# A two-layer hybrid block on one core: residual stream with tokens on partitions instead of features

## The chip, the core and the metric

The kernel runs on one core of a Trainium2 chip. The metric is the device time of one execution in microseconds (us); the figure for the kernel before is the median of three timed runs. A profile is one further execution, recorded instruction by instruction; its span runs from the first to the last instruction.

## What is computed

Two layers work on 256 latent tokens `x` and 256 context tokens `ctx`, 1024 features each. A layer is a half feed-forward step, a token mixing (gated linear attention, a 2D Fourier transform, latent attention, merged by gates) and a second half feed-forward step. The last layer drops the context after its mixing. Each of the six steps has this frame, cut from the reference:

```
def _rmsnorm(x, g):
    xf = x.astype(jnp.float32)
    y = xf * lax.rsqrt(jnp.mean(xf * xf, axis=-1, keepdims=True) + EPS)
    return (y * g.astype(jnp.float32)).astype(x.dtype)
def _half_ffn(x, mod, g_pre, g_post, wg, wu, wd):
    shift, scale, gate = mod
    h = _rmsnorm(x, g_pre) * (1 + scale) + shift
    y = (jax.nn.silu(h @ wg) * (h @ wu)) @ wd
    return x + 0.5 * gate * _rmsnorm(y, g_post)
```

`wg` and `wu` are 1024 x 2816, `wd` is 2816 x 1024, and the output projection of the mixing, `w_out`, is 1024 x 1024. `shift`, `scale` and `gate` come from a modulation, one vector for the context and one for the latents.

## The kernel before, in words

All activations lie with features on the partitions: 8 tiles of 128 features by 512 tokens, the context in columns 0 to 255, the latents in 256 to 511. Every product is done in float32r with both operands split into a high and a low part, so one block of 128 x 128 weights costs three matmuls: weights-high by activations-high, weights-high by activations-low, weights-low by activations-high (`acc`). The weights are stationary, the tokens move: 512 columns for both streams, 256 for one.

Weights stream through `Stream`: SP issues loads of 512 KB into four raw buffers, ACT copies the high part (line 140), DVE subtracts for the low part (line 141), in pieces of 512 columns, up to 8 or 9 pieces ahead of use. The modulation vectors (`mod_chunk`, line 292) are made by DVE beside the first two feed-forward steps, from weights that pass through the same four buffers.

The six steps are called f0, mixer and f1 of layer 0 and layer 1 here; each ends in `down` (the product by `wd`, tiles named `d`, or by `w_out`, tiles named `o`). `down` makes one output tile of 128 features at a time. The last one (two for `o`) is made first for the context half and then for the latent half, 256 columns each, so that the norms of the context half lie beside the products of the latent half; `dense_pair` does the same with the first two or four tiles of the next step. Between the two lie, per half, `postnorm` and `prenorm`: sums of squares over the partitions by fp32 matmuls against ones (tiles `png`, `pnc`, `qnc`), a power of -0.5 on POOL (`pnr`, `qnr`), a broadcast of the result over the partitions by another matmul (`pnb`, `qnb`), then DVE, ACT and POOL apply it. In layer 1 only the latents pass `o` and f1, 256 columns at a time.

Each engine takes its instructions in a fixed order, which a scheduler writes when the program is built; an instruction that waits holds up all behind it on its engine.

Of the kernel before, what the change touches and what calls it, by code (L numbers as in the profile page):

```python
# [16 lines left out]
L = 2  # L17
# [15 lines left out]
PER_ATT = 4  # L33

# [6 lines left out]
# chunks in the order in which each direction's state passes them, but for the last  # L41
# [3 lines left out]
# columns of the tables of the 2D transform  # L45
# [136 lines left out]
class K:  # L182
# [10 lines left out]
    def pools(self, ctx):  # L193
        P = lambda **k: ctx.enter_context(self.tc.tile_pool(**k))
        self.const = P(name="const", bufs=1)
        self.raw_p = P(name="raw", bufs=RAW_BUFS)
        self.c_p = P(name="c", bufs=C_BUFS)
        self.f_p = P(name="f", bufs=3)
        self.s_p = P(name="s", bufs=7)
        self.t_p = P(name="t", bufs=3)  # L200
        self.v_p = P(name="v", bufs=6)
        self.mm_p = P(name="mm", bufs=3, space=PSUM)
        self.aux_p = P(name="aux", bufs=5, space=PSUM)
# [4 lines left out]
    def rows(self, n, name, dt=F32):  # L208
        """n tiles [128, 512], two in each buffer."""
# [24 lines left out]
    def setup(self):  # L234
# [5 lines left out]
        self.x = c.tile([128, NT, 512], F32, name="x")  # L240
        nc.scalar.dma_start(self.cond, self.io["cond"])
        for j in range(4):
            nc.sync.dma_start(self.x[:, 2 * j:2 * j + 2, :], self.io["x"][:, 2 * j:2 * j + 2, :])
# [14 lines left out]
    def cond_rows(self):  # L258
        """silu of both conditions along the free axis, for the modulation."""
# [7 lines left out]
    def mod_finish(self, l, i, m, ts=slice(0, NT)):  # L267
        """Adds the bias and folds the weights of the norms into scale and gate."""
# [12 lines left out]

    def mod_chunk(self, l, i):
        """One of the nine modulation vectors of both conditions, feature-major: [128, tile, cond]."""
        nc = self.nc
        m = self.const.tile([128, NT, 2], F32, name=f"m{l}_{i}")
        rs = [1] if l == L - 1 and i > 4 else [0, 1]
        if len(rs) == 1:
            nc.vector.memset(m, 0.0)
# [9 lines left out]
        self.modv[l][i] = m  # L298

    def first_mod(self, t, m2, ps):  # L300
        """Shift and scale of the first norm, for one tile of features."""
# [18 lines left out]
    def start(self):  # L320
        """The first norm and the first tiles of the first FFN, one tile of features at a time, as
        their modulation arrives."""
# [3 lines left out]
        m2 = [self.const.tile([128, NT, 2], F32, name=f"m0_{a}") for a in range(2)]  # L326
        self.modv[0][0:2] = m2
        sqs = []
        for j in range(4):
            sq, xj = self.c([2, 512], "xsq"), self.x[:, 2 * j:2 * j + 2, :]  # L330
            if j % 2:
                nc.vector.tensor_tensor(sq, xj, xj, ALU.mult)
            else:
                nc.scalar.activation(sq, xj, AF.Square)
            sqs += [sq[:, 0, :], sq[:, 1, :]]
        tot = self.sums(sqs, "pn", 512)
        self.first_mod(0, m2, mps)
        bc = self.rstd_of(tot, 1.0 / D, "pn")
        pg = [self.mm("pg") for _ in range(M0)]
        pu = [self.aux("pu") for _ in range(M0)]  # L340
        for t in range(NT):
            if t:
                self.first_mod(t, m2, mps)
            for hf in range(2):
                self.pre_tile(0, 0, hf, t, bc[:, 256 * hf:256 * hf + 256])
# [9 lines left out]
    def rstd(self, sqs, invd, name):  # L355
        """1/sqrt(mean + eps) of the tokens on all partitions; sqs: squares to be summed."""
        return self.rstd_of(self.sums(sqs, name), invd, name)

    def sums(self, sqs, name, n=256):
        """Sums over the features, tokens on the partitions."""  # L360
        nc = self.nc
        col = self.ones[:, 0:1]
        if len(sqs) == NT:
            gps = self.aux(name + "g")
            for j in range(NT):
                g = 32 * (j % 4)
                nc.tensor.matmul(gps[g:g + 32, 0:n], lhsT=self.ones[:, 0:32], rhs=sqs[j], start=j < 4, stop=j >= 4)
            part = self.t(name + "s") if n == 256 else self.s(name + "s")
            nc.vector.tensor_copy(part, gps[:, 0:n])
            sqs, col = [part], self.cst[:, C_32:C_32 + 1]  # L370
        cps = self.aux(name + "c")
        for c in range(n // 128):
            for i, sq in enumerate(sqs):
                nc.tensor.matmul(cps[:, c:c + 1], lhsT=sq[:, 128 * c:128 * c + 128], rhs=col,
# [19 lines left out]
    def pre_stats(self, hf):  # L394
        nc = self.nc
        sl = slice(256 * hf, 256 * hf + 256)
        sqs = []
        for j in range(4):
            sq = self.s("xsq", (2, 256))
            nc.scalar.activation(sq, self.x[:, 2 * j:2 * j + 2, sl], AF.Square)  # L400
            sqs += [sq[:, 0, :], sq[:, 1, :]]
        return self.rstd(sqs, 1.0 / D, "pn")

    def pre_tile(self, l, which, hf, t, bc):
# [5 lines left out]
        if t % 2 == 0 or t == 1:  # L410
            nc.vector.scalar_tensor_tensor(tmp, self.x[:, t, sl], A, bc, ALU.mult, ALU.mult)
            nc.scalar.activation(hi, tmp, AF.Identity, bias=B)  # L412
            nc.vector.scalar_tensor_tensor(lo, tmp, B, hi.bitcast(F32), ALU.add, ALU.subtract)
        else:
            nc.vector.tensor_tensor(tmp, self.x[:, t, sl], bc, ALU.mult)
            nc.scalar.activation(tmp, tmp, AF.Identity, bias=B, scale=A)
            nc.scalar.copy(hi, tmp)
            nc.gpsimd.tensor_tensor(lo, tmp, hi.bitcast(F32), ALU.subtract)  # L418

    def prenorm(self, l, which, hf):  # L420
        bc = self.pre_stats(hf)
        for t in range(NT):
            self.pre_tile(l, which, hf, t, bc)

    def postnorm(self, hf, out=False):
        nc = self.nc
        sl = slice(256 * hf, 256 * hf + 256)
        bc = self.rstd([q[:, sl] for q in self.ysq], 1.0 / D, "qn")
        for j in range(4):
            yj, xj = self.y[j][:, :, sl], self.x[:, 2 * j:2 * j + 2, sl]  # L430
            nc.vector.tensor_tensor(yj, yj, bc.unsqueeze(1).broadcast_to([128, 2, 256]), ALU.mult)
            (nc.vector if j >= 2 else nc.gpsimd).tensor_tensor(xj, xj, yj, ALU.add)
            if out:
                nc.sync.dma_start(self.io["out"][:, 2 * j:2 * j + 2, :], xj)
# [7 lines left out]
    def dense(self, key, rhi, rlo, t0, name):  # L442
        """One tile of 128 output features by the tokens from t0, over len(rhi) tiles of inputs."""
# [8 lines left out]
    def dense_pair(self, keys, t0, names):  # L452
        """Several tiles over the whole width, first for the context, then for the latent tokens."""
        if t0:
            return [self.dense(k, self.hi, self.lo, t0, n) for k, n in zip(keys, names)]
        out, blocks = [], []
        for key, n in zip(keys, names):
            self.W.unit(key, 1024)
            blocks.append([self.W.next() for _ in range(NT)])
            out.append((self.aux if len(out) % 2 and len(keys) > 3 else self.mm)(n))  # L460
        for hf in range(2):
            sl = slice(256 * hf, 256 * hf + 256)
            for ps, bl in zip(out, blocks):
# [789 lines left out]
```

## Time and profile before

| | |
|---|---|
| median of three runs | 2275.65 us (2273.53 to 2286.22) |
| span of the profiled execution | 2269.7 us |
| mean granted TensorE clock | 0.979 of full |
| busy: PE, DVE, ACT, POOL | 2174.9, 1325.8, 883.0, 254.2 us |
| read from HBM | 294.93 MB |

The profiled execution has no time of its own beside its span; the span lies 5.95 us under the median of the runs. PE's busy time counts overlapping matmuls once, each with its way through the array, so it tells that PE is rarely empty, not how fast it goes.

### The profile page before, as it was taken

The numbers are of one execution on the slowest core, as the hardware profiler recorded it, in microseconds if no ns is written. First come the engines' busy times: TensorE is split into PE (matmuls) and PEld (weight loads), VectorE is DVE, ScalarE is ACT, GpSimd is POOL, SyncE is SP. The second block draws the span as 40 slices with busy tenths as digits, with TensorE's granted clock in tenths as the row PEclk, the third lists the DMA queues.
The fourth block names the chain that finished last, engine by engine and source line by source line (L and its number), as shares of the span: only waits on it lengthen the run. The fifth ranks groups of instructions, "written<-read, shape, count | busy, mean of one in ns | idle before, by whom it ended". The sixth has DMA issues, their size and how long they took to land.

```text
span 2269.7 us, 34594 instructions
## 1 busy us (share of the span) xinstructions
PE 2174.9 (96%) x13686; PEld 1842.6 (81%) x13686; DVE 1325.8 (58%) x2568; ACT 883.0 (39%) x1759; POOL 254.2 (11%) x227
## 2 busy tenths in 40 slices
PE   7999999899999999999999999999998999998998
PEld 5788777677777788888888878888887788998998
DVE  4877687567665734377765553333225677665553
ACT  3332222454344523442232343323325445555452
POOL 0000001233120100200000020000002332101001
PEclk9999999899999999999999999999999999998999
DMA  8555466221111223245556623232321322453552
GB/s 300 192 182 197 159 202 207 86 93 57 41 60 56 88 81 111 75 158 176 195 197 218 214 77 112 75 111 71 119 90 47 121 69 89 152 183 129 186 188 92
DMA packets 87587, 298.23 MB, mean 131 GB/s; under 512 B 9664, under 2 KB 14016, under 8 KB 87424
## 3 DMA queue, kind: packets, MB, share of 16 engines
q1 hardware_dynamic: 85760, 291.54, 38.8%
q10 hardware_dynamic: 1664, 4.48, 0.6%
q8 instruction: 107, 1.75, 0.3%
q14 instruction: 56, 0.46, 0.1%
HBM read 294.93 MB, written 1.05 MB: 130 GB/s over the span
## 4 chain that ended last, share of the span: by engine, by line
PE 66%; DVE 13%; DMA 9%; ACT 4%; issue 4%; POOL 3%; ACTq 0%; DVEq 0%; POOLq 0%
DMA raw<-wmod 8%; PE d L438 5%; PE d L440 5%; PE d L439 5%; PE pu L439 4%; PE pu L440 4%; PE pu L438 3%; PE pg L439 3%; PE pg L440 3%; PE pg L438 3%; DVE junk L292 3%; PE ga L440 3%; PE ga L438 3%; PE ga L439 3%; DVE raw L292 3%
## 5 line engine op out<-in xcount | busy, mean ns | idle before, releaser
L141 DVE TENSOR_TENSOR w<-raw,w 128x512 fp32r<-128x512 f32 (+1 forms) x840 | 536.5, 685 | 246.9 <-ACT w L140 244.0
L140 ACT CAST w<-raw 128x512 fp32r<-128x512 f32 (+1 forms) x840 | 460.8, 605 | 244.7 <-DMA raw<-wd 73.3
L292 DVE SCALAR_TENSOR_TENSOR raw<-raw,cbc 128x1024 f32<-128x1024 f32 x128 | 159.7, 1248 | 50.7 <-DMA raw<-wmod 48.5
L292 DVE SCALAR_TENSOR_TENSOR junk<-raw,cbc 128x1024 f32<-128x1024 f32 x96 | 120.2, 1252 | 88.6 <-DMA raw<-wmod 88.4
L510 POOL TENSOR_TENSOR dq<-dq 128x512 f32<-128x512 f32 (+1 forms) x24 | 30.5, 1269 | 1143.2 <-ACT dq L483 1143.2
L543 DVE TENSOR_TENSOR sg<-sg,pu 128x512 f32<-128x512 f32 (+1 forms) x88 | 54.3, 618 | 155.2 <-PE pu L440 151.8
L483 ACT ACTIVATE dq<-d 128x512 f32<-128x512 f32 (+1 forms) x35 | 17.9, 511 | 175.4 <-PE d L440 175.4
L438 PE MATMUL ga<-h01h,w 128*128 128x512 f32 x192 | 76.0, 396 | 0.0
L542 ACT ACTIVATE sg<-pg 128x512 f32<-128x512 f32 (+1 forms) x88 | 47.5, 540 | 72.8 <-PE pg L440 72.8
L440 PE MATMUL ga<-h01h,w 128*128 128x512 f32 x192 | 75.4, 393 | 0.0
L439 PE MATMUL ga<-h01l,w 128*128 128x512 f32 x192 | 75.0, 391 | 0.0
L439 PE MATMUL pg<-h02l,w 128*128 128x512 f32 (+1 forms) x192 | 71.8, 376 | 1.7 <-POOL h02l L418 1.6
L438 PE MATMUL pu<-h02h,w 128*128 128x512 f32 (+1 forms) x192 | 72.5, 378 | 0.0
L439 PE MATMUL pu<-h02l,w 128*128 128x512 f32 (+1 forms) x192 | 72.3, 377 | 0.0
L440 PE MATMUL pu<-h02h,w 128*128 128x512 f32 (+1 forms) x192 | 72.3, 377 | 0.0
L440 PE MATMUL pg<-h02h,w 128*128 128x512 f32 (+1 forms) x192 | 72.0, 376 | 0.1
L438 PE MATMUL pu<-h10h,w 128*128 128x512 f32 (+1 forms) x192 | 72.0, 375 | 0.0
L439 PE MATMUL pg<-h10l,w 128*128 128x512 f32 (+1 forms) x192 | 71.5, 373 | 0.4 <-POOL h10l L418 0.4
L438 PE MATMUL pg<-h02h,w 128*128 128x512 f32 (+1 forms) x192 | 71.6, 376 | 0.2 <-ACT w L140 0.2
L439 PE MATMUL pu<-h10l,w 128*128 128x512 f32 (+1 forms) x192 | 71.7, 374 | 0.0
L438 PE MATMUL pg<-h00h,w 128*128 128x512 f32 x176 | 69.4, 394 | 2.4 <-ACT h00h L412 2.1
L440 PE MATMUL pu<-h10h,w 128*128 128x512 f32 (+1 forms) x192 | 71.7, 373 | 0.0
(528 smaller groups left out, 6208.9 us busy)
## 6 DMA issues: line engine op xcount, KB each, us to landing
raw<-wgu SPq DMA_DIRECT2D x170, 512.0 KB, 4.5
raw<-wmod SPq DMA_DIRECT2D x128, 512.0 KB, 4.3
raw<-win SPq DMA_DIRECT2D x92, 512.0 KB, 3.6
raw<-wd SPq DMA_DIRECT2D x64, 448.0 KB, 4.0
raw<-wd SPq DMA_DIRECT2D x32, 512.0 KB, 4.5
raw<-wm SPq DMA_DIRECT2D x16, 512.0 KB, 7.3
raw<-wbr SPq DMA_DIRECT2D x16, 512.0 KB, 3.6
raw<-wout SPq DMA_DIRECT2D x16, 512.0 KB, 4.5
```

Of the source, the lines that this page charges most:

```text
L140: nc.scalar.copy(hi, w)
L141: nc.vector.tensor_tensor(lo, w, hi.bitcast(F32), ALU.subtract)
L292: nc.vector.scalar_tensor_tensor(w if r else self.junk, w, 1.0, self.cbc[r], ALU.mult, ALU.mult, accum_out=m[:, t, r:r + 1])
L438: nc.tensor.matmul(ps, lhsT=hi, rhs=rhi, start=first, stop=False)
L439: nc.tensor.matmul(ps, lhsT=hi, rhs=rlo, start=False, stop=False)
L440: nc.tensor.matmul(ps, lhsT=lo, rhs=rhi, start=False, stop=last)
L483: nc.scalar.activation(sq[:, sl], ps[:, sl], AF.Square)
L510: nc.gpsimd.tensor_tensor(accq[:, t0:512], accq[:, t0:512], sq[:, t0:512], ALU.add)
L542: nc.scalar.activation(sg[:, t0:512], pg[:, t0:512], AF.Silu)
L543: nc.vector.tensor_tensor(sg[:, t0:512], sg[:, t0:512], pu[:, t0:512], ALU.mult)
```

## The change

The residual `x` is kept with tokens on the partitions: four tiles of 128 tokens by 1024 features. In `down` the activations are now the stationary operand and the weights move, 512 output features at a time: for each half `h` of the features and each of the 22 (or 8) input tiles, four token tiles (two in layer 1's `o` and last `d`) get three matmuls. The last `hold` input tiles of the second half are held back and done token tile by token tile, so that tiles 0 to 3 end one after the other. ACT squares a finished PSUM tile with a running sum along the free axis, DVE multiplies it by the gate, which now lies along the free axis and is fetched through DRAM (`gate_rows`). `residual` finishes a token tile: two small DVE steps with a power on POOL between, the update of `x`, the sum of squares of the new `x`, another power, and the normed rows `n`. These go back to features on partitions by transposes on PE (`turned`, `turn_tile`), and `pre_tile` applies scale and shift from PSUM. The matmuls for sums and broadcasts of these norms are gone. `dense_pair` now walks the input tiles outermost, issues the latent half's transposes and `pre_tile` (`self.late`) inside its context half, and takes three tiles instead of two at the start of a mixer.

```
+    def residual(self, j, ss, out):
+        r = self.norm_of(ss[:, 0:1], ss[:, 1:2])
+        sx = self.v("sx", 2)
+        for h in range(2):
+            sl = slice(512 * h, 512 * h + 512)
+            xj = self.x[:, j, sl]
+            nc.vector.scalar_tensor_tensor(xj, self.y[j][:, sl], r, xj, ALU.mult, ALU.add)
             if out:
...
+                nc.scalar.activation(self.sink[:, sl], xj, AF.Square, scale=D ** -0.5, accum_out=sx[:, h:h + 1])
...
+        r = self.norm_of(sx[:, 0:1], sx[:, 1:2])
+        n = self.c([D], f"n{j}")
+        nc.vector.tensor_scalar(n, self.x[:, j, :], r, None, ALU.mult)
+        return n
...
+        def mul(ps, kt, w, j):
+            sl = slice(128 * j, 128 * j + 128)
+            hi, lo = ahi[kt][:, sl], alo[kt][:, sl]
+            nc.tensor.matmul(ps, lhsT=hi, rhs=w[0], start=kt == 0, stop=False)
+            nc.tensor.matmul(ps, lhsT=hi, rhs=w[1], start=False, stop=False)
+            nc.tensor.matmul(ps, lhsT=lo, rhs=w[0], start=False, stop=kt == n - 1)
...
+        def evac(ps, j, h):
+            sl = slice(512 * h, 512 * h + 512)
+            nc.scalar.activation(self.sink[:, sl], ps, AF.Square, scale=D ** -0.5, accum_out=ss[j][:, h:h + 1])
+            nc.vector.tensor_tensor(y[j][:, sl], ps, g[j // 2][:, sl], ALU.mult)
...
+        for j in tiles:
+            for kt, w in held:
+                mul(ps[j], kt, w, j)
+            evac(ps[j], j, 1)
+            ns[j] = self.residual(j, ss[j], nxt is None)
+            if j == 2 and t0 == 0 and nxt:
+                turned = [self.aux("pt", (2, 256)) for _ in range(4)]
+                self.turn_tile(turned, 0, ns[0])
+            yield
...
+            if t0 == 0:
+                self.turn_tile(turned, 1, ns[1])
+                half(0, turned)
+            self.late = lambda: half(1, self.turned([ns[2], ns[3]]))
```

`norm_of` is a small DVE step and the power on POOL; `hold` is 6 in f0 and f1, 8 in the mixers.

At the seam from f0 to the mixer of layer 1, DVE's queue held these rows before. `qnv` belongs to the norm of the latent half of `d`'s last tiles, `dy` and `x` to the residual of the context half, `pnv` to its next norm, `h11l` is the low part of the mixer's input.

```order
L382 TENSOR_SCALAR qnv<-qnc 128x2
L141 TENSOR_TENSOR w_13740<-raw_13614,w_13740 128x512
L141 TENSOR_TENSOR w_13754<-raw_13646,w_13754 128x512
L141 TENSOR_TENSOR w_13769<-raw_13646,w_13769 128x512
L431 TENSOR_TENSOR dy_13016<-dy_13016,qnb 128x2x256
L431 TENSOR_TENSOR dy_13017<-dy_13017,qnb 128x2x256
L431 TENSOR_TENSOR dy_13018<-dy_13018,qnb 128x2x256
L431 TENSOR_TENSOR dy_13019<-dy_13019,qnb 128x2x256
L432 TENSOR_TENSOR x<-x,dy_13018 128x2x256
L432 TENSOR_TENSOR x<-x,dy_13019 128x2x256
L369 COPY pns<-png 128x256
L382 TENSOR_SCALAR pnv<-pnc 128x2
```

Now the same place on DVE reads, for the last two of the four token tiles (the first two stand ahead of it in the same way):

```order
L529 TENSOR_TENSOR dy_12838<-d,gr_12882 128x512
L445 SCALAR_TENSOR_TENSOR nv<-ss_12842 128x1
L457 SCALAR_TENSOR_TENSOR x<-dy_12838,nr,x 128x512 x2
L445 SCALAR_TENSOR_TENSOR nv<-sx 128x1
L466 TENSOR_SCALAR n_13607<-x,nr 128x1024
L529 TENSOR_TENSOR dy_12839<-d,gr_12882 128x512
L445 SCALAR_TENSOR_TENSOR nv<-ss_12843 128x1
L457 SCALAR_TENSOR_TENSOR x<-dy_12839,nr,x 128x512 x2
L445 SCALAR_TENSOR_TENSOR nv<-sx 128x1
L466 TENSOR_SCALAR n_13654<-x,nr 128x1024
L438 TENSOR_SCALAR pnt<-pt,m_4_9526,m_3_9203 128x256
L439 TENSOR_TENSOR h11l_13500<-pnt,h11h_13496 128x256
```

The whole chain of the latents' tiles 2 and 3 stands ahead of the first low part `h11l` of the context half; before, only the context half's own norms did.

On PE the last rows of `d` and the first of the mixer's pair at the same seam were, before:

```order
L387 MATMUL pnb<-cst,pnr 128x128 x2
L440 MATMUL d<-a20h_12941,w_13643 128x256
L438 MATMUL d<-a20h_12941,w_13643 128x256
L439 MATMUL d<-a20l_12942,w_13643 128x256
L440 MATMUL d<-a20h_12941,w_13643 128x256
L374 MATMUL qnc<-cst,dq 128x1 x4
L438 MATMUL zx<-h11h_13805,w_13657 128x256
```

and now, from the last three products of token tile 3 on:

```order
L522 MATMUL d<-w_13423,a20h_12761 128x512
L523 MATMUL d<-w_13423,a20h_12761 128x512
L524 MATMUL d<-w_13423,a20l_12762 128x512
L428 MATMUL pt<-cst,n_13572 128x128 x8
L428 MATMUL pt<-cst,n_13607 128x128 x2
L471 MATMUL zx<-h11h_13496,w_13440 128x256
L471 MATMUL zk<-h11h_13496,w_13472 128x256
L471 MATMUL zk<-h11h_13496,w_13480 128x256
L428 MATMUL pt<-cst,n_13654 128x128 x2
L472 MATMUL zx<-h11l_13500,w_13440 128x256
```

Between the last product of `d` and the first of the mixer there are no products left for PE to do, only transposes; the fp32 sums and broadcasts are gone.

## Rows read from the trace of the kernel before

**Rows 1.** The page, busy time by engine, with its share and instructions:

```profile
PE 2174.9 (96%) x13686; PEld 1842.6 (81%) x13686; DVE 1325.8 (58%) x2568; ACT 883.0 (39%) x1759; POOL 254.2 (11%) x227
```

**Rows 2.** Timeline of PE, `o` of layer 0: start us, us, what; ten products of 512:

```profile
902.75 0.39 PE L438 MATMUL o<-mh,w 128*128 128x512 f32 x1
...
904.79 0.39 PE L438 MATMUL o<-mh,w 128*128 128x512 f32 x1
```

**Rows 3.** Timeline of PE, last `d`: 23 products of 256:

```profile
2199.78 0.28 PE L438 MATMUL d<-a14h,w 128*128 128x256 f32 x1
...
2202.42 0.28 PE L439 MATMUL d<-a20l,w 128*128 128x256 f32 x1
```

**Rows 4.** Busy time (instructions) by engine, clock, DMA, at the five seams:

```profile
388.93:447.07 58.14, 48.01 (x309) 40.79 (x307) 37.94 (x73) 25.70 (x53) 16.29 (x15) 0.85 0.35 111
935.39:992.34 56.95, 51.79 (x369) 46.39 (x368) 31.12 (x60) 28.36 (x56) 14.69 (x15) 0.88 0.21 67
1315.56:1372.81 57.25, 51.89 (x398) 46.69 (x396) 36.77 (x68) 30.36 (x62) 14.98 (x15) 0.97 0.27 89
1695.15:1744.15 49.00, 41.22 (x309) 35.92 (x308) 27.88 (x55) 23.83 (x49) 14.59 (x15) 0.97 0.21 65
2051.31:2065.86 14.55, 7.39 (x38) 4.06 (x37) 6.23 (x12) 3.78 (x8) 3.91 (x4) 0.68 0.12 38
```

**Rows 5.** Groups of instructions by shape: busy us, mean ns of one:

```profile
L141 DVE TENSOR_TENSOR w<-raw,w 128x512 fp32r<-128x512 f32 x736 | 485.2, 702 | 227.7 <-ACT w L140 225.1
L543 DVE TENSOR_TENSOR sg<-sg,pu 128x512 f32<-128x512 f32 x66 | 45.2, 684 | 119.3 <-PE pu L440 116.3 <-ACT sg L542 2.9
L755 DVE SCALAR_TENSOR_TENSOR tg<-tg,br 128x512 f32<-128x512 f32 x24 | 16.5, 686 | 56.9 <-PE br L440 56.9
L1029 DVE TENSOR_SCALAR pr<-pr,rr 128x512 f32<-128x512 f32 x32 | 17.5, 546 | 0.2
L1029 DVE TENSOR_SCALAR pr<-pr,rr 128x256 f32<-128x256 f32 x16 | 5.6, 348 | 0.3
L415 DVE TENSOR_TENSOR pnt<-x,pnb 128x256 f32<-128x256 f32 x33 | 13.6, 413 | 0.8 <-POOL h02l L418 0.2 <-POOL h11l L418 0.2 <-POOL h10l L418 0.2
L483 ACT ACTIVATE dq<-d 128x512 f32<-128x512 f32 x21 | 12.5, 597 | 126.1 <-PE d L440 126.1
L1027 ACT ACTIVATION_READ_ACCUMULATOR pr<-sc,nb 128x1 f32 x48 | 9.2, 193 | 0.0
L400 ACT ACTIVATE xsq<-x 128x512 f32<-128x512 f32 x36 | 22.0, 629 | 30.8 <-POOL x L432 30.2 <-DVE x L432 0.5
L384 POOL TENSOR_TENSOR pnr<-pnv,cst 128x4 f32<-128x4 f32 x1 | 1.3, 1285 | 16.8 <-DVE pnv L382 16.8
L1047 PE MATMUL pt<-cst,pr 128*128 128x128 f32 x160 | 23.0, 275 | 1.3 <-DVE nb L1024 1.3
```

**Rows 6.** Timeline of all engines after the last product:

```profile
2257.98 0.28 PE L440 MATMUL d<-a20h,w 128*128 128x256 f32 x1
...
2259.66 0.16 DVE L382 TENSOR_SCALAR qnv<-qnc 128x2 f32<-128x2 f32 x1 [15.46 <-PE qnc L374]
2259.90 0.71 POOL L384 TENSOR_TENSOR qnr<-qnv,cst 128x2 f32<-128x2 f32 x1 [8.26 <-DVE qnv L382]
...
2263.81 2.00 DVE L432 TENSOR_TENSOR x<-x,dy 128x512 f32<-128x512 f32 x2
```

**Rows 7.** Timeline of PE, first products of layer 1's f1, eleven of 256:

```profile
2066.24 0.41 PE L438 MATMUL pu<-h12h,w 128*128 128x256 f32 x1
...
2068.37 0.41 PE L440 MATMUL pg<-h12h,w 128*128 128x256 f32 x1
```

**Rows 8.** As rows 4, for most of `d` of layer 0's f0:

```profile
281.00:395.00 114.00, 111.71 (x510) 92.00 (x509) 88.56 (x145) 33.07 (x68) 10.21 (x6) 1.00 0.63 204
```

**Rows 9.** Timeline of PE, the first product of the kernel:

```profile
24.12 0.50 PE L438 MATMUL pg<-h00h,w 128*128 128x512 f32 x1 [0.95 <-ACT h00h L412]
```

More of the change, by code (lines that the diff above doesn't have):

```diff
@@ L298, in mod_chunk, with gate_rows @@
         self.modv[l][i] = m
+        if i % 3 == 2:
+            rows = self.dram_p.tile([32, 128], F32, tag="rows", name=f"rows{l}_{i}")
+            tr = self.t("rowt", 32)
+            nc.vector.transpose(tr, whole)
+            nc.sync.dma_start(rows.rearrange("c (b q) -> b c q", q=32), tr)
+            self.rows_of[l, i] = rows
+    def gate_rows(self, l, i, rs):
+        rows = self.rows_of[l, i]
+        out = {}
+        for r in rs:
+            out[r] = self.c([D], f"gr{r}")
+            row = rows[16 * r:16 * r + NT, :].rearrange("t q -> (t q)").unsqueeze(0)
+            self.nc.sync.dma_start(out[r], row.broadcast_to([128, D]))
+        return out
     def first_mod(self, t, m2, ps):
@@ L392, in new_h, with turned, turn_tile, pre_tile @@
         self.hi, self.lo = self.split_rows(NT, name)
[L394 to L404, printed above, removed]
+    def turned(self, ns):
+        out = [self.aux("pt", (2, 256)) for _ in range(4)]
+        for j, n in enumerate(ns):
+            self.turn_tile(out, j, n)
+        return out
+    def turn_tile(self, out, j, n):
+        for t in range(NT):
+            self.nc.tensor.transpose(out[t // 2][:, t % 2, 128 * j:128 * j + 128], n[:, 128 * t:128 * t + 128], self.ident)
+    def pre_tile(self, l, which, hf, t, n):
         nc = self.nc
@@ L420, in prenorm @@
[L420 to L425, printed above, removed]
-        nc = self.nc
[L427 to L432, printed above, removed]
-            if out:
-                nc.sync.dma_start(self.io["out"][:, 2 * j:2 * j + 2, :], xj)
+        nc.scalar.activation(hi, n, AF.Identity, bias=B, scale=A)
@@ new lines, in evac @@
+        def evac(ps, j, h):
+            sl = slice(512 * h, 512 * h + 512)
+            nc.scalar.activation(self.sink[:, sl], ps, AF.Square, scale=D ** -0.5, accum_out=ss[j][:, h:h + 1])
+            nc.vector.tensor_tensor(y[j][:, sl], ps, g[j // 2][:, sl], ALU.mult)
+        for h in range(2):
+            ps = {j: (self.mm if h and j < 3 else self.aux)(name) for j in tiles}
+            held = []
+            for kt in range(n):
+                if kt % 2 == 0:
+                    self.W.unit(key(h, kt // 2), 1024)
+                w = self.W.next(512)
+                if h and kt >= n - hold:
+                    held.append((kt, w))
+                else:
+                    for j in tiles:
+                        mul(ps[j], kt, w, j)
+                if g is None and kt == 1:
+                    g = self.gate_rows(*gate, self.halves(t0))
+                if kt % 2:
+                    yield
+            if h == 0:
+                for j in tiles:
+                    evac(ps[j], j, h)
@@ new lines, in down, with half @@
+        ns = {}
+        turned = None
+        if nxt:
+            self.new_h(f"h{nxt[0]}{nxt[1]}")
+        for j in tiles:
+            for kt, w in held:
+                mul(ps[j], kt, w, j)
+            evac(ps[j], j, 1)
[3 more added lines that the diff above has]
+                self.turn_tile(turned, 0, ns[0])
+            yield
+        def half(hf, banks):
+            for t in range(NT):
+                self.pre_tile(*nxt, hf, t, banks[t // 2][:, t % 2, :])
```

192 lines of the change are left out of this document (73 added, 119 removed).

## Prediction

> **What bounds the kernel now.** I read the page first: PE is busy 96% of the span [rows 1], so only what shortens PE's own queue, or an emptiness of it, counts. Busy time doesn't give PE's pace, since matmuls overlap; the timeline does. Ten products of 512 columns start within 2.04 us, 0.227 us apart [rows 2]; 23 of 256 within 2.64 us, 0.120 apart [rows 3]. So two half-width products cost 0.240 us where one of full width costs 0.227. Between the seams PE keeps that pace almost without a gap. The seams are where it doesn't: I take for each the stretch from the first half-width product of the old step to the end of the half-width products of the new one [rows 4] and take off the products. At f0 to mixer of layer 0, 58.1 us hold 132 + 96 half products and 7 of full width that belong to the next tile, 28.9 us: 29.2 are something else. Mixer to f1: 57.0 less 288 half products (34.6) leaves 22.4. f1 to layer 1: 57.3 less 324 (38.9) leaves 18.4. f0 to mixer of layer 1: 49.0 less 235 (28.2) leaves 20.8. Before the last f1 there are no half-streams to cover anything: 14.55 us without any product. After the last product, at 2257.98 [rows 6], 11.7 us pass to the end of the span at 2269.7. These 117 us, fp32 sums, waits for norms and slow clock (0.85 and 0.88 at two seams, 0.68 at the fifth), are what the change can win or lose; the middle of the steps it hardly touches.
>
> **Products.** Layer 1's `d` goes from 528 half products (63.4 us) to 264 full ones (59.9): -3.5. Its `o` from 192 to 96: -1.2. The split last tiles of `d` in three steps, 132 half to 66 full each: -0.9 x 3; of `o` in layer 0, 96 to 48: -0.6. The third tile in both pairs turns 24 full products into 48 half ones: +0.3 x 2. Sum -7.4 us. That activations are stationary and weights move is not new to PE: the value projections already do so, in the same shape, so I keep 0.227.
>
> **The chain of a token tile.** At the seam each token tile now needs, on DVE, in queue order: the gated copy from PSUM (0.684, as line 543), a small step (0.16 [rows 6]), a wait for POOL's power (0.71, plus 0.08 and 0.05 of hand-over [rows 6]), two updates of `x` (0.686 each, as line 755), a wait for ACT's second square and its accumulator (0.63 + 0.19), a small step, another power, and the normed row: 0.546 for 512 elements against 0.348 for 256 makes about 0.94 for 1024 [rows 5]. Sum 0.68 + 0.16 + 0.84 + 1.37 + 0.82 + 0.16 + 0.84 + 0.94 = 5.8, with the hand-over to and from ACT 5.9 us. While DVE waits for POOL or ACT, the next tile's copy stands behind the waiting row and can't start: the rows of the order shown ahead go tile by tile. PE delivers a token tile of `d` each 18 x 0.227 = 4.1 us, of `o` each 24 x 0.227 = 5.4. DVE is therefore slower than PE, falls behind from tile to tile, and the context half's `pre_tile`, which PE needs next, stands behind tile 3's chain.
>
> **The seams after.** From the end of tile 0 on PE: square and accumulator 0.9 with hand-over, four chains 23.6, the first `pre_tile` 0.8 (two steps of at most 0.41): 25.3 us. To it come the weight splits that stand among the chains, 0.70 each [rows 5]: six at the first seam, four at the third, none at the others. PE's own held products end 12.3 us after tile 0 for `d`, 16.3 for `o`. PE stands without products for 29.5 - 12.3 = 17.2 us, 25.3 - 16.3 = 9.0, 28.1 - 12.3 = 15.8 and 25.3 - 12.3 = 13.0. Of 32 transposes eight lie in that emptiness. The other 24 I cost at 0.144 (23.0 us for 160 [rows 5]), 3.5 us. After such an emptiness the clock is at the lower level: the fifth seam shows 0.68, and the products behind it start 0.213 apart instead of 0.120 [rows 7]. I take 20 such products, 1.9 us. So the four seams cost 22.6, 14.4, 21.2 and 18.4 us. The first gets 8 us more: in `d` of f0 DVE is busy 88.6 of 114 us beside the modulation [rows 8], and the change puts eight PSUM copies on it (5.5) and makes it stand for ACT's squares in the middle (some 2.4); the bounds are 0, if the 25 idle us take it, and the full 8. Before the last f1: 0.9 + 2 x 5.9 + 8 transposes (1.2) + 0.8 less 5.4 of held products, 9.3 us, with the slow clock as before.
>
> Against before: +1.4, -8.0, +2.8, -2.4, -5.3; sum -11.5 us.
>
> **End.** After the last product: 0.9 + 0.68 + 0.16 + 0.84 + 1.37 = 4.0 us to the last update (tile 2's chain without the second norm is 4.0 too, so it doesn't hold up tile 3), then as long as before from DVE's last end at 2265.81 [rows 6] to 2269.7: 7.9 instead of 11.7, with the last product's own 0.3 us 8.2. -3.5.
>
> **Start.** Transposes and their copies replace 16 fp32 sums ahead of the first product at 24.12 [rows 9]; squares, power and modulation stay. I leave it at 0; its bounds are -2 and +3 us, half of a tile chain either way. The gate rows are two more loads of 512 KB for each `down`, issued at its second input tile and wanted half a `down` later (60 us in `d`, 22 in `o`, 11 in layer 1's `o`): nothing, while the loads ahead of them on SP don't stand; a wait there would be hidden by the up to eight pieces split ahead. The removed sums on POOL and ACT lay off the path and give nothing of their own.
>
> Sum: -7.4 - 11.5 - 3.5 = -22.4 us, from a span of 2269.7 to 2247.3. With the 5.95 us between span and median unchanged: 2253 us, range of its own 2240 to 2264.
>
> **Rivals.** *The chain is dearer, and the change loses.* Place: POOL and the hand-overs in each tile's chain. Each us more per tile costs four at four seams and two at the fifth, 18 us. The gain is gone at +1.24 us per tile, and the kernel slower by over 0.5% at +1.9. For it: the same power took 1.285 in one row [rows 5]; with 0.57 more at both powers the time is 2253 + 20.5 = 2274. Eight hand-overs dearer by 0.25 each, with DVE and ACT on both sides, make 2.0: 2289. Against it: the hand-overs seen are 0.05 to 0.08 [rows 6].
>
> *The slow clock lasts.* If PE kept the lower level through the first half of each pair, 72 or 96 products, 336 in all, at 0.093 more, less what I took: +23.6, 2277. For it: the emptiness of 9 to 17 us is longer than what the seams had, and the pair runs behind `pre_tile`s. Against it: at the fifth seam, with 14.55 us, the clock was back soon enough for a mean of 0.979.
>
> *Transposes cost their own duration*, 0.275 us each [rows 5], since they don't overlap: 24 x 0.131 at four seams and 1.0 at the fifth, +13.6, 2267. Against it: 160 of them cover 23.0 us, not 44. The Trainium skill (TensorE: Matmul & The Clock Gate, Part 4: PE-mode transpose) gives about 275 ns for a transpose within a kernel, a rule against this change. By that figure as a price the time would be this rival's; the trace has the same 275 ns, as a duration that overlaps.
>
> *DVE isn't held.* If the chains of successive tiles overlapped, so that a tile took only DVE's busy 3.8 us, PE would wait for one chain, 0.9 + 5.9 + 0.8 = 7.6 us, at the four seams: less by 9.6, 1.4, 8.2 and 5.4, 2228. Against it: the order on DVE.
>
> **Numbers.** Likeliest as summed 0.61; dearer chain but not slower 0.10, slower 0.11; slow clock 0.07; transposes 0.04; overlap 0.07. About 0.5% (11 us) is what a measurement of this kernel can tell from no change: faster is below 2264. That takes the likeliest and the overlap, 0.68; the dear chain, the clock and the transposes end within it, 0.21; slower 0.11. The range leaves out the overlap and the slower chain: 2235 to 2278.
>
> **What would show it.** Right: full products 0.227 apart in `d` and `o`; on PE, before each pair, 9 to 17 us without a product that end with `pre_tile` (`h..l`) on DVE; DVE waiting for POOL `nr` and ACT `sx` eight times a seam; some 8 us after the last product. Wrong: DVE's tiles 7 us and more apart; a clock well under 0.97; PE waiting for weights inside `d`; SP standing at the gate rows so that raw loads come late.

## The result, and the profile after

The changed kernel takes 2219.16 us (median of four, 2217.11 to 2227.98) where the kernel before takes 2275.03: a ratio of 0.9749, interval 0.9719 to 0.9778, 56 us less. The forecast was 2253 us, 22 us less; the measured time lies below its range.

The profiled execution is the slowest of the four: span 2226.2 us, clock 0.975, while the others have spans of 2218.1, 2216.6 and 2215.3 at 0.982 to 0.983. It lost some 9 us in the middle of layer 1's mixer (last section). Against the 2269.7 us of before the trace therefore shows 43.5 us, and without that loss 52 to 53. The rest up to 56 is on the side of before: with the 1.8 us by which a run's time exceeds its span here, its profiled execution lay 3.5 us under its median.

PE, the matmul engine, stays the bound (DVE is the vector engine, ACT the scalar engine, POOL GpSimd). Page, busy time, as in [rows 1]:

```profile
PE 2127.2 (96%) x12928; PEld 1801.6 (81%) x12928; DVE 1352.9 (61%) x2642; ACT 858.0 (39%) x1701; POOL 163.2 (7%) x176
```

The groups of the token tile's chain, by shape, busy us and mean ns of one; they answer to [rows 5]:

```profile
L529 DVE TENSOR_TENSOR dy<-d,gr 128x512 f32<-128x512 f32 x28 | 19.0, 688 | 75.9 <-ACT sink L528 75.6
L457 DVE SCALAR_TENSOR_TENSOR x<-dy,nr,x 128x512 f32<-128x512 f32 x28 | 19.8, 749 | 10.1 <-POOL nr L446 10.1
L466 DVE TENSOR_SCALAR n<-x,nr 128x1024 f32<-128x1024 f32 x18 | 13.6, 753 | 12.9 <-POOL nr L446 12.9
L446 POOL TENSOR_TENSOR nr<-nv,cst 128x1 f32<-128x1 f32 x38 | 20.9, 550 | 1496.9 <-DVE nv L445 1496.9
L428 PE MATMUL pt<-cst,n 128*128 128x128 f32 x176 | 26.8, 301 | 19.6 <-DVE n L466 10.8 <-DVE dy L529 8.1 <-ACT n L370 0.8
```

The stretches of PE from the last product of the old step to the first of the new one, at the five seams (columns as in [rows 4]):

```profile
400.77:412.96 12.19, 2.29 (x14) 1.57 (x13) 7.58 (x15) 6.09 (x15) 2.20 (x4) 0.70 0.25 86
929.60:935.00 5.40, 1.26 (x10) 0.93 (x8) 2.75 (x6) 2.58 (x7) 0.69 (x2) 0.97 0.00 0
1302.70:1313.20 10.50, 1.27 (x10) 0.94 (x8) 6.36 (x13) 4.03 (x11) 1.76 (x4) 0.69 0.16 51
1680.10:1688.20 8.10, 1.68 (x13) 1.11 (x11) 4.57 (x9) 4.03 (x11) 1.30 (x4) 0.84 0.00 0
2021.60:2030.00 8.40, 3.08 (x19) 2.51 (x17) 4.10 (x9) 2.70 (x7) 1.66 (x3) 0.82 0.00 0
```

Less the last product's own 0.23 us, PE is without products for 12.0, 5.2, 10.3, 7.9 and 8.2 us; forecast were 17.2 (and 8 more of backlog), 9.0, 15.8, 13.0 and 9.3. Only transposes run in them, 8 to 16 each. Why they are shorter is seen at the fourth seam. DVE, from token tile 1's gated copy on (with start and duration):

```profile
1673.38 0.68 DVE L529 TENSOR_TENSOR dy<-d,gr 128x512 f32<-128x512 f32 x1
1673.98 0.15 DVE L445 SCALAR_TENSOR_TENSOR nv<-ss 128x1 f32<-128x1 f32 x1
1674.86 1.41 DVE L457 SCALAR_TENSOR_TENSOR x<-dy,nr,x 128x512 f32<-128x512 f32 x2 [0.73 <-POOL nr L446]
1677.12 0.16 DVE L445 SCALAR_TENSOR_TENSOR nv<-sx 128x1 f32<-128x1 f32 x1 [0.85 <-ACT sink L461]
1678.01 0.75 DVE L466 TENSOR_SCALAR n<-x,nr 128x1024 f32<-128x1024 f32 x1 [0.73 <-POOL nr L446]
1678.68 0.68 DVE L529 TENSOR_TENSOR dy<-d,gr 128x512 f32<-128x512 f32 x1
...
1688.60 0.75 DVE L466 TENSOR_SCALAR n<-x,nr 128x1024 f32<-128x1024 f32 x1 [0.73 <-POOL nr L446]
1689.27 0.54 DVE L438 TENSOR_SCALAR pnt<-pt,m,m 128x256 f32<-128x256 f32 x1
1689.84 0.42 DVE L439 TENSOR_TENSOR h11l<-pnt,h11h 128x256 fp32r<-128x256 f32 x1
```

The chains stand one behind the other, with the waits that were forecast, but a tile takes 5.30 us (1673.38 to 1678.68) and not 5.9. PE and ACT at the same place:

```profile
1680.06 0.39 PE L524 MATMUL d<-w,a20l 128*128 128x512 f32 x1
1680.29 1.03 PE L428 MATMUL pt<-cst,n 128*128 128x128 f32 x8
1684.71 0.44 PE L428 MATMUL pt<-cst,n 128*128 128x128 f32 x2 [3.39 <-DVE dy L529]
1688.18 0.58 PE L471 MATMUL zx<-h11h,w 128*128 128x256 f32 x1 [3.03 <-ACT h11h L437]
...
1690.32 0.58 PE L472 MATMUL zx<-h11l,w 128*128 128x256 f32 x1 [0.22 <-DVE h11l L439]
```

```profile
1686.96 0.63 ACT L461 ACTIVATE sink<-x 128x512 f32<-128x512 f32 x1
...
1687.59 0.55 ACT L437 ACTIVATE h11h<-pt,m,m 128x256 fp32r<-128x256 f32 x1
```

PE's first product starts 0.4 us ahead of tile 3's normed row on DVE. It needs ACT's high part alone, and on ACT that row stands behind tile 3's squares only, not behind its second power and normed row.

### The profile page after: what moved, and what is told of

The parts are those of the page before. It is cut to its first block, busy times and chain, and to the rows that moved or that the text cites. A ratio compares the mean times of both kernels' runs of the same rounds, so it can differ in the third digit from the quotient of the medians.

```text
span 2226.2 us, 33002 instructions
## 1 busy us (share of the span) xinstructions
PE 2127.2 (96%) x12928; PEld 1801.6 (81%) x12928; DVE 1352.9 (61%) x2642; ACT 858.0 (39%) x1701; POOL 163.2 (7%) x176
## 4 chain that ended last, share of the span: by engine, by line
PE 69%; DVE 13%; DMA 8%; ACT 5%; issue 4%; POOL 2%; ACTq 0%; POOLq 0%; DVEq 0%
DMA raw<-wmod 6%; PE d L523 6%; PE d L524 6%; PE d L522 6%; PE pg L472 4%; PE pu L472 4%; PE pu L473 4%; PE pg L473 4%; PE pu L471 4%; PE pg L471 4%; PE ga L473 3%; PE ga L471 3%; PE ga L472 3%; DVE w L142 3%; DVE junk L300 2%
## 5 line engine op out<-in xcount | busy, mean ns | idle before, releaser
L142 DVE TENSOR_TENSOR w<-raw,w 128x512 fp32r<-128x512 f32 (+2 forms) x824 | 533.0, 692 | 139.9 <-ACT w L141 137.3
L141 ACT CAST w<-raw 128x512 fp32r<-128x512 f32 (+2 forms) x824 | 460.0, 611 | 303.8 <-DMA raw<-wd 73.3
L446 POOL TENSOR_TENSOR nr<-nv,cst 128x1 f32<-128x1 f32 x38 | 20.9, 550 | 1496.9 <-DVE nv L445 1496.9
L471 PE MATMUL pg<-h10h,w 128*128 128x512 f32 (+1 forms) x192 | 72.3, 377 | 9.3 <-ACT h10h L437 9.3
L789 DVE SCALAR_TENSOR_TENSOR tg<-tg,br 128x512 f32<-128x512 f32 (+1 forms) x48 | 26.5, 552 | 75.6 <-PE br L473 67.6
L473 PE MATMUL pg<-h10h,w 128*128 128x512 f32 (+1 forms) x192 | 72.0, 375 | 0.0
L473 PE MATMUL pu<-h10h,w 128*128 128x512 f32 (+1 forms) x192 | 71.7, 373 | 0.0
```

What stands on the lines that cost most here:

```text
L141: nc.scalar.copy(hi, w)
L142: nc.vector.tensor_tensor(lo, w, hi.bitcast(F32), ALU.subtract)
L471: nc.tensor.matmul(ps, lhsT=hi, rhs=rhi, start=first, stop=False)
L473: nc.tensor.matmul(ps, lhsT=lo, rhs=rhi, start=False, stop=last)
L789: nc.vector.scalar_tensor_tensor(x, x, 1.0, ps[:, t0:512], ALU.add, ALU.mult)
```

## The experiments

All medians are of four or five runs; "before" in the ratios is the kernel before on the same chip. The gaps are PE's times without products at the first four seams, read as above; "pair" is the time from there to the end of the first 144 half-width products (17.3 us at full pace), with the transposes that stand among them. Stretches with the same code differ from trace to trace: the first `d` starts between 278.5 and 282.6 us in these thirteen, and layer 0's mixer takes 493.4 to 496.5 us from the end of its pair to the next gap. So of a difference of 2 or 3 us between two medians only what the gaps and pairs show is put down to an edit.

| kernel | us | ratio (interval) | gaps | pair |
|---|---|---|---|---|
| changed | 2219.2 | 0.9749 (0.9719–0.9778) | 12.0 5.2 10.3 7.9 | 22.6 22.7 23.1 23.0 |
| e1 normed row twice | 2229.4 | 0.9811 (0.9784–0.9838) | 13.4 7.1 12.3 9.9 | 23.9 23.0 22.7 23.4 |
| e2 no power | 2204.6 | 0.9696 (0.9672–0.9720) | 8.4 4.7 7.0 4.7 | 22.6 22.4 22.6 22.7 |
| e3 rows in the waits | 2212.7 | 0.9731 (0.9705–0.9756) | 6.1 1.5 5.7 3.3 | 28.9 25.5 24.2 24.7 |
| e4 ten held | 2212.7 | 0.9732 (0.9708–0.9756) | 11.1 5.2 5.2 5.2 | 23.5 23.3 22.6 22.6 |
| e5 chains written overlapped | 2216.9 | 0.9736 (0.9705–0.9768) | 11.4 5.2 8.2 7.9 | 23.4 23.5 23.5 22.5 |
| e6 = e5, rows in the waits | 2209.0 | 0.9707 (0.9676–0.9737) | 4.7 1.5 3.4 3.3 | 28.5 25.4 23.6 24.7 |
| e7 = e6, late transposes | 2211.6 | 0.9714 (0.9683–0.9746) | 4.3 1.5 3.3 3.4 | 28.3 25.3 24.3 25.4 |
| e8 more copies | 2230.2 | 0.9793 (0.9762–0.9824) | 12.0 5.2 10.3 7.9 | 22.6 23.3 23.4 22.5 |
| e9 = e6, ten held | 2205.4 | 0.9683 (0.9659–0.9706) | 3.7 1.5 1.5 1.5 | 31.6 25.3 23.0 23.9 |
| e10 = e6, POOL's rows | 2205.4 | 0.9689 (0.9667–0.9710) | 4.5 1.5 3.3 3.3 | 28.1 24.8 24.6 25.0 |
| e11 = e9 and e10 | 2201.2 | 0.9668 (0.9646–0.9690) | 3.1 1.5 1.5 1.5 | 29.7 25.4 22.6 24.1 |
| e12 spread rows | 2221.3 | 0.9749 (0.9729–0.9768) | 12.5 5.2 10.3 7.9 | 22.6 23.5 22.7 22.7 |

**e1: a dearer chain.**

```diff
         nc.vector.tensor_scalar(n, self.x[:, j, :], r, None, ALU.mult)
+        nc.vector.tensor_scalar(n, self.x[:, j, :], r, None, ALU.mult)
         return n
```

> The normed row of each token tile is written twice, which adds 0.67 us of DVE to each chain (start to start of that row and the next in the changed kernel) and nothing else. Theory: at the seams PE waits for DVE's chains one after the other, so each us per tile costs 4 us at four seams and 2 at the fifth. 18 x 0.67 = +12.1 us against the changed kernel, about 2231 us. Rival: the seams came out shorter than forecast because the chain is no longer what PE waits for (PE's own held products and ACT's rows decide); then it stays under +4 us.

10.2 us more than the changed kernel. DVE's tiles at the fourth seam, where the second row landed behind the next tile's copy:

```profile
1680.43 0.68 DVE L530 TENSOR_TENSOR dy<-d,gr 128x512 f32<-128x512 f32 x1
1681.03 0.74 DVE L467 TENSOR_SCALAR n<-x,nr 128x1024 f32<-128x1024 f32 x1
...
1686.39 0.68 DVE L530 TENSOR_TENSOR dy<-d,gr 128x512 f32<-128x512 f32 x1
```

5.96 us a tile instead of 5.30, and the gaps grow by 1.4, 1.9, 2.0 and 2.0: three times 0.66, not four, since the first product waits for three normed rows only. The low part waits for the fourth. The gap before the last f1 grows by 1.6, so the five gaps grow by 8.9 in sum, and the pairs by 1.6. What DVE's chain takes is paid by PE, as the prediction had it.

**e2: a cheaper chain.** The power of both norms is left out, a constant takes its place.

```diff
-        nc.gpsimd.tensor_tensor(r, v, self.cst[:, C_MH:C_MH + 1], ALU.pow)
+        nc.vector.tensor_scalar(r, v, 0.0, 0.25, ALU.mult, ALU.add)
```

> The power on POOL is left out of every token tile's two norms: DVE writes the constant 0.25 in its place, so the output isn't normed. A tile's chain loses two hand-overs to POOL and back, 0.88 and 0.89 us become 0.15 each, 1.45 us per tile net of the 0.15 that DVE's own row takes, say 1.2 to 1.45. Theory (DVE's chains in a row): 18 x 1.2 to 1.45 = -22 to -26 us, 2193 to 2198 us, less where PE's own products (4.1 us per tile) become the limit. Rival (transposes and slow clock decide, or POOL's waits are hidden by ACT's squares): less than -6 us.

14.6 us less, between the theory and its rival. At the fourth seam:

```profile
1659.87 0.69 DVE L529 TENSOR_TENSOR dy<-d,gr 128x512 f32<-128x512 f32 x1 [17.05 <-ACT sink L528]
1660.48 0.15 DVE L445 SCALAR_TENSOR_TENSOR nv<-ss 128x1 f32<-128x1 f32 x1
1660.66 0.15 DVE L446 TENSOR_SCALAR nr<-nv 128x1 f32<-128x1 f32 x1
1660.85 1.42 DVE L457 SCALAR_TENSOR_TENSOR x<-dy,nr,x 128x512 f32<-128x512 f32 x2
...
1664.24 0.69 DVE L529 TENSOR_TENSOR dy<-d,gr 128x512 f32<-128x512 f32 x1
```

A tile takes 4.37 us: 0.93 less, where 1.2 to 1.45 were expected: from a norm's first small row to the row that uses the result 0.37 to 0.46 us still pass, not 0.15. The gaps behind the down projections fall by 3.6, 3.3 and 3.2. Behind the output projection the gain is only 0.5: there PE delivers a tile each 5.4 us, the changed kernel's 5.30 is already below that, and what remains is the way of the last tile alone.

**e3: the context half's rows in the waits of tile 3.**

```diff
         r = self.norm_of(ss[:, 0:1], ss[:, 1:2])
+        fill()
...
+        fill()
         r = self.norm_of(sx[:, 0:1], sx[:, 1:2])
+        fill()
...
+            if j == 3 and t0 == 0 and nxt:
+                self.turn_tile(turned, 1, ns[1])
+                todo = [(0, t) for t in range(NT)]
+                def fill():
+                    hf, t = todo.pop(0)
+                    self.pre_tile(*nxt, hf, t, turned[t // 2][:, t % 2, :])
```

> The modulated rows of the context half (which need token tiles 0 and 1 alone) are put into the three waits of token tile 3's chain instead of behind it. Theory: PE stands still at four seams because these rows are queued behind tile 3 on DVE and on ACT, though their data are there. The first half-width products with both parts then come 4 to 5 us sooner: -16 to -20 us, about 2201. Rival: the wait only moves, since the latent half needs tile 3, whose chain becomes longer: 0 to -5 us, with PE standing at the transposes of tiles 2 and 3 instead.

6.5 us less. The gaps fall by 5.9, 3.7, 4.6 and 4.6 as the theory says, so the rows' place in the queues was what PE waited for. But the pairs become longer by 6.3, 2.8, 1.1 and 1.7, the rival's way. PE at the first seam, second half of the pair:

```profile
427.31 0.39 PE L475 MATMUL zx<-h01h,w 128*128 128x256 f32 x1 [0.17 <-ACT h01h L437]
430.68 0.39 PE L476 MATMUL zx<-h01l,w 128*128 128x256 f32 x1 [2.75 <-DVE h01l L439]
```

and DVE there:

```profile
424.27 4.90 DVE L142 TENSOR_TENSOR w<-raw,w 128x512 fp32r<-128x512 f32 x8
429.08 0.54 DVE L438 TENSOR_SCALAR pnt<-pt,m,m 128x256 f32<-128x256 f32 x1
```

Eight weight splits stand ahead of the latent half's rows.

**e4: ten input tiles held.** `HOLD_D` is 10 instead of 6.

> In the down projections the last 10 input tiles are held back for each token tile instead of 6, so PE has 10 x 9 products = 20.4 us after tile 0 instead of 12.3. Theory: the emptiness at the three seams behind a down projection (12.0, 10.3 and 7.9 us) shrinks by up to 8.1 us each, and with it some of the slow clock: -22 to -28 us, about 2194. Rival: the four more pairs of weight blocks occupy buffers of the common pool, so the next step's weights can't be split ahead and PE waits for them at the pair instead: -10 us to +5.

6.5 us less. That is inside the rival's range, but by neither account: PE waits for no weights at the pairs, and the gaps stop at 5.2 at the third and fourth seam. 5.2 is what the output projection had all along, the way of tile 3 from PE's last product to ACT's high part. At the first seam 11.1 remain, since tile 0 now ends before the modulation's rows do:

```profile
390.50 0.19 DVE L277 TENSOR_TENSOR m<-m,vec 128x16 f32<-128x16 f32 x1
390.59 0.68 DVE L529 TENSOR_TENSOR dy<-d,gr 128x512 f32<-128x512 f32 x1
```

**e5, e6, e7: chains written overlapped.** The tile's chain becomes a generator with stops behind the first norm, the updates, the second norm and the normed row, and the next tile's copy and first norm are issued between them; e6 also issues the context half's rows there, e7 moves the transposes of tiles 2 and 3 on PE.

```diff
+            if prev:
+                next(prev)
             evac(ps[j], j, 1)
-            ns[j] = self.residual(j, ss[j], nxt is None)
+            cur = self.residual(j, ss[j], nxt is None, ns)
+            if prev:
+                next(prev, None)
+            next(cur)
+            if prev:
+                next(prev, None)
```

```diff
-                if hf == 0 and kt == NT - 3:
+                if hf == 0 and kt == NT - 1:
```

> The chains of successive token tiles are written overlapped: the next tile's gated copy and its first norm's small step stand in the waits of a tile's second norm, so that a tile takes DVE about 3.9 us (two updates 1.33, wait for the squares and the power 1.85, normed row 0.67) instead of 5.3. Theory: in the changed kernel DVE's order makes the tiles wait for each other; with 3.9 under PE's 4.1 per tile of a down projection the emptiness falls to one tile's own path, 5.2 us (what the output projection shows already): up to -6.8, 0, -5.1 and -2.7 us at four seams, in sum -10 to -15 against the changed kernel (2217 without its disturbed mixer). Rival: the squares now stand in a row on ACT and the tiles wait there: 0 to -4 us.

> As the overlapped chains, and the context half's modulated rows stand ahead of and in the waits of token tile 3's chain. Theory: the 5.2 us that then remain before each pair are the wait for tile 3, which the context half doesn't need; its first products come 2 to 4 us after PE's last product, -6 to -12 us against the overlapped kernel. Rival: as with the context half's rows alone, the latent half gives it back, since tile 3's chain becomes longer and weight splits stand ahead of its rows: within 3 us of the overlapped kernel.

> As the kernel with both, and the transposes of token tiles 2 and 3 stand on PE behind the last of the context half's products, not behind the sixth of eight input tiles. Theory: PE stood there with 18 half-width products (2.2 us) queued behind them; where tile 3 is late they now run first: up to -2.2 us at each of four seams, -4 to -9 us. Rival: tile 3 is in time by then, and PE now waits for the modulated row of the latent half behind its transposes (some 1.5 us a seam): +3 to +6 us.

e5 moved the time by 2 us and says nothing on its question: on DVE the next copy still stands behind the normed row, tile by tile 5.3 us apart at the third and fourth seam; at the third the gap fell to 8.2 as the four weight splits that stood between the tiles (some 2.4 us) are gone from there. Code written in another order did not give the order that was meant, and no run here has chains that overlap on DVE. e6 is 8 us faster than e5; against e3 it is 3.6 faster, and its gaps and pairs are 4.8 shorter. e7 is 2.6 us slower than e6, within the noise, and its pairs are 1.1 longer in sum, not shorter: the transposes' place is not what they wait for.

**e8 and e12: is there room on DVE in the first down projection?** e8 writes each of the first half's copies five times, in a lump; e12 adds 16 single rows of the same length to the second half of the first `down`.

```diff
                     evac(ps[j], j, h)
+                    for _ in range(4 if t0 == 0 and name == "d" else 0):
+                        nc.vector.tensor_tensor(y[j][:, 0:512], ps[j], g[j // 2][:, 0:512], ALU.mult)
```

```diff
+                if h and name == "d" and t0 == 0 and gate == (0, 2) and kt < 16:
+                    nc.vector.tensor_tensor(self.junk[:, 0:512], g[0][:, 0:512], g[0][:, 512:1024], ALU.mult)
```

> In the three down projections of all tokens each of the four gated copies of the first 512 output features is written five times: 16 more DVE rows of 0.6 us, 9.6 us, in the middle of each. Theory: the waits of DVE for the modulation's weights (16.1 us in the first down projection) take them, as they took the change's own copies, and the spare 1.7 us before tile 0's copy takes the rest: 0 to +3 us. Rival: the first seam's DVE is full, and only luck hid the forecast 8 us: +7 to +10 us there, nothing at the others.

> The same 9.6 us of DVE as with the more copies, but in the first down projection alone and one row of 0.6 us at a time, at each of 16 input tiles of its second half of features; the rows compute nothing that is used. Theory: in this stretch DVE stands 16 to 19 us for weights of the modulation and of the step, and tile 0's copy has 1.7 us to spare, so small rows find room, neither the splits nor the seam wait for them, and the time stays within 3 us of the changed kernel (2217 to 2219). That would show why the forecast backlog of 8 us (5.5 us of copies, 2.4 of standing) did not come. Rival: the modulation's rows are pushed back one for one, tile 0's chain starts that much later, and the emptiness at the first seam grows from 12.0 to 18 to 20 us: +6 to +8.

e8 is 11 us slower, but not at the seam, whose gap stays at 12.0: PE stands in the middle of that `d` (and hardly in the others).

```profile
360.62 0.80 PE L523 MATMUL d<-w,a4h 128*128 128x512 f32 x1 [8.05 <-DVE w L142]
```

The copies are a lump of 12 us ahead of seven weight splits, more than the pieces split ahead can cover. The same 9.6 us in single rows (e12) leave the time within 2 us of the changed kernel's, and the gap at 12.5. What DVE waited for between 279 us and tile 0's copy (total, times, longest), in the changed kernel:

```profile
DVE junk L300 <- DMA raw<-wmod: 16.1, 12, 3.3
```

and with the spread rows:

```profile
DVE junk L300 <- DMA raw<-wmod: 9.3, 8, 2.1
```

The waits for the modulation's weights shrank by 6.8 us, and the 1.7 us that DVE had to spare ahead of tile 0's copy are used up too: the rows found room, and just that much. e8 and e12 differ in the rows' place as well as in their size (first half and second half of `d`); the two were not tried apart.

**e9, e10, e11: both waits, and less DVE.** e9 is e6 with ten held; e10 is e6 with three of the eight modulated rows of each half (input tiles 3, 5 and 7) made as in the kernel before, by ACT and POOL; e11 is both.

```diff
+        if t % 2 and t > 1:
+            nc.scalar.activation(tmp, n, AF.Identity, bias=B, scale=A)
+            nc.scalar.copy(hi, tmp)
+            nc.gpsimd.tensor_tensor(lo, tmp, hi.bitcast(F32), ALU.subtract)
+            return
```

> The kernel that puts the context half's rows ahead of and into tile 3's chain, with 10 instead of 6 input tiles of the down projections held back. Theory: the two edits bear on different waits (the held products cover DVE's lag of four chains, the rows' place takes tile 3 off the path), so at the seams behind a down projection PE's first product comes some 1.5 us after its last, as it already does behind the output projection, instead of 3.3 to 4.7, and tile 3's rows are earlier for the latent half: -6 to -10 us against that kernel (2209). Rival: the four more blocks held keep buffers, and DVE's weight splits, which then come later, stand ahead of the latent half's rows: within 3 us.

> The same kernel (6 input tiles), and of every four modulated rows the three odd ones behind the first take the way of the kernel before: ACT makes the modulated value and its high part, POOL the low part. Theory: in the pair behind a seam DVE is the bound (16 pairs of modulated rows of 0.9 to 1.0 us, 7 weight splits of 0.6 and tile 3's chain stand in a row while PE has 18 us of products): six of sixteen rows less are 5.8 us of DVE, -2 to -4 us at each of four seams, 2195 to 2201. Rival: POOL takes 0.73 us and more for a row and ACT a second pass, so PE waits for these rows instead: 0 to +6 us.

> Both at once. Theory: what each gives adds up, 2188 to 2196. Rival: whichever of the two does nothing alone does nothing here either.

3.6 us less than e6 in e9, 3.6 in e10, 7.8 in both: the medians add up, each below its theory, but only e9's part is shown to come from its edit. Its last three gaps are 1.5 us as expected, its first is 3.7 and the pair behind it takes 31.6; gaps and pairs together are 3.1 us below e6's. e10's are the same as e6's in sum, 115.1 us, and what it gains stands in stretches where nothing was meant to change: 3.0 us in the rest of layer 0's mixer, where e11, with the same rows, takes as long as e6. So at six held tiles less DVE work is not shown to gain anything; with ten held (e11 against e9) gaps and pairs are 2.6 us shorter. e11 is the best kernel of the study, 18 us faster than the changed one. PE there at the fourth seam:

```profile
1671.90 0.39 PE L532 MATMUL d<-w,a20l 128*128 128x512 f32 x1
1672.13 1.03 PE L428 MATMUL pt<-cst,n 128*128 128x128 f32 x8
1673.58 0.38 PE L479 MATMUL zx<-h11h,w 128*128 128x256 f32 x1 [0.42 <-ACT h11h L442]
```

## Why the prediction was wrong

The direction, the place and, in the main, the mechanism were right; the sum was less than half of the gain. The step that failed is "The seams after", in two places of it, and a third is smaller: it put 76.6 us and 8 of backlog on the four seams, and they took 61.2.

| term | forecast | profiled |
|---|---|---|
| products of layer 1's `d` and `o` | -4.7 | -5.0 |
| four seams, all that isn't product | 22.6, 14.4, 21.2, 18.4 | 18.2, 11.5, 17.0, 14.5 |
| backlog at the first of them | 8 | 0 |
| gap before the last f1 | 9.3 | 8.2 |
| after the last product | 8.2 | 7.3 |
| start to first `d` | 0 | -2.0 |
| layer 1's mixer, this execution | 0 | +9 |

A profiled seam is its gap, the time that the pair takes beyond 17.3 us, and 0.9 for the eight transposes that stand among the held products: 12.0 + 5.3 + 0.9 at the first.

**Products: right.** Layer 1's `d` runs from 2159.3 to 2218.9, 59.6 us where it took 63.3 (forecast 59.9), its `o` 21.6 instead of 23.0. With stationary activations products still start 0.227 us apart (59.6 for 263 steps).

**"Sum 0.68 + 0.16 + 0.84 + ... = 5.8": mis-sized.** By starts the parts are 0.60, 0.88, 2.26, 0.89 and 0.67 against 0.68, 1.00, 2.19, 1.00 and 0.94, and 0.1 for hand-overs. The largest error is the normed row: "about 0.94 for 1024", carried on from [rows 5], is 0.75 long, and the next row starts 0.67 after it. The two powers come next, 0.23 together: one column takes POOL 0.55, and the 0.71 was of two. The rest is overlap: the copy is 0.68 long, and the next row starts 0.60 after it, some 0.08 that the prediction counted twice by adding durations, which it was careful not to do for PE. Four chains are 2.4 us shorter, two 1.2. The price per us was nearly right: e1 cost 10.2 us for 0.66 a tile, 15 per us where 18 were forecast. Because 5.30 lies under PE's 5.4 per tile of `o`, where 5.9 would have been over it, the second seam is of another kind: there nothing queues, and 5.2 us are the last tile's way, which e1 lifts to 7.1 by crossing 5.4.

**"The context half's `pre_tile`, which PE needs next, stands behind tile 3's chain": half wrong.** True on DVE, for the low part. On ACT the high part waits for the squares alone, so the first products start some 2 us sooner than forecast and a few run before the low part comes. e3 shows that the order of these rows is what PE stands for: moved, they take 3.7 to 5.9 us from each gap.

**"The first gets 8 us more": wrong.** The bounds were 0 and 8, and the text took 8. In the changed kernel the modulation's last row ends at 387.06 and tile 0's copy starts at 388.78, with 1.72 us to spare. Before and after:

```profile
397.00 0.17 DVE L274 TENSOR_TENSOR m<-m,vec 128x16 f32<-128x16 f32 x1
```

```profile
386.87 0.19 DVE L277 TENSOR_TENSOR m<-m,vec 128x16 f32<-128x16 f32 x1
388.78 0.69 DVE L529 TENSOR_TENSOR dy<-d,gr 128x512 f32<-128x512 f32 x1 [1.72 <-ACT sink L528]
```

The added rows did not push the modulation back. Counted from the first `d` (281.05 before, 279.03 now) it ends 8 us sooner, after 108.0 us instead of 116.1, and after 107.5 to 109.8 in the ten experiments that add no DVE rows to the middle of `d`. DVE's waits for its weights fell from 20.1 to 16.1 us there, so part of the added work went into them, the lower bound's own reason; what else made it end sooner no run shows. e12 shows that up to some 10 us more of single rows would have fitted. e8 shows the condition: in a lump the same rows cost 11 us, at another place than the one forecast.

**Transposes and slow clock: nearly right.** 5.4 us per seam were forecast. Beyond the half-width products the pairs take 5.3 to 5.8, and the transposes among the held products the 0.9: 6.2 to 6.7. Eight transposes take 0.79 us of PE there, 0.10 each, and eleven in a row in the first pair 1.12, though one is 0.30 long, so the rival of their own duration falls; the figure of the Trainium skill (TensorE: Matmul & The Clock Gate, Part 4: PE-mode transpose), about 275 ns, lies near the duration of 0.30 and is no price here. The slow clock didn't last: in each pair 20 to 23 products start some 0.21 us apart before the pace is 0.12 again, as was taken. Behind the longest gap (the granted clock is the third number from the end; 0.50 is the lower level):

```profile
412.96:418.00 5.04, 4.25 (x20) 3.95 (x19) 4.83 (x12) 3.08 (x7) 0.00 (x0) 0.50 0.34 106
424.00:430.00 6.00, 5.86 (x49) 5.65 (x48) 6.00 (x14) 3.44 (x7) 0.00 (x0) 1.00 0.90 320
```

What the pairs take beyond the forecast, about 1 us each, includes waits for the low part `h..l`, 0.2 to 1.1 us a pair, that had no term.

**The other rivals.** The dearer chain is refuted by its own rows (5.30). "DVE isn't held" would have given 2228, near the measured time, but its mechanism isn't there: the tiles stand in a row on DVE, with PE delivering one each 4.1 us.

**End and start.** After the last product 7.3 us pass instead of 8.2. The first product is 1.3 us later, as the bounds allowed, but the first step ends 2.0 sooner: before, PE had waited 1.23 us for a weight at 258 us and does not now. The 2.0 is no gain of the change that could be told from noise: the first `d` starts at 281.05 before and between 278.5 and 282.6 in the thirteen traces since.

The +9 is the loss against e12's trace; against the 83.0 us of the kernel before it is 8.1. With the first mixer some 2 us shorter, which is within its spread, the terms make the 43.5 us of the trace to within 1.

## What to carry to other kernels

Price each row of a chain on an in-order engine at its own shape, sum by starts and not by durations, and compare it with the rate at which the engine before delivers: just under that rate the queue vanishes and only the last piece's way is left. At a seam, list for each engine where the row that the next product needs is queued; data that are ready behind somebody else's wait are what costs, and when such a row is moved, look at what then stands ahead of the next one. Room on an engine depends on how the rows are put in: single rows fit into waits for loads, a lump in front of rows that feed the bound does not.

## What was not expected of the hardware

One execution lost 9 us with no change of the program. In the profiled execution of the changed kernel PE stood in the scan of layer 1's mixer for nothing that the profile shows:

```profile
1816.37 0.35 PE L949 MATMUL dl<-q,kq 64*32 64x32 f32 x13 [2.42 <-issue]
```

From there the granted clock was 0.50 and products ran at half pace (0.43 us instead of 0.227) until 1832:

```profile
1820.00:1824.00 4.00, 4.00 (x16) 3.10 (x14) 0.88 (x2) 0.29 (x1) 0.00 (x0) 0.50 0.65 212
```

So the stretch of that mixer took 91.1 us,

```profile
1760.50:1851.60 91.10, 84.16 (x960) 73.50 (x958) 55.37 (x163) 36.02 (x86) 21.69 (x24) 0.85 0.21 68
```

where e12, which has the same program there, took 81.9:

```profile
1760.50:1842.40 81.90, 77.17 (x959) 67.94 (x958) 55.24 (x163) 36.05 (x86) 21.70 (x24) 0.94 0.24 76
```

A stop of 2.4 us in a stretch of small matmuls, with the clock's lower level behind it, was followed by a loss of four times its length. In the traces of the twelve experiments the rest of this mixer, from its pair to the next gap, takes 299.1 to 301.0 us, and 310.5 here. What stopped PE stays open.
